# Side work of a scan held in queues: a bidirectional RWKV-7 and convolution layer on one core

## The chip, the cores and the metric

The kernel runs on one core of a Trainium2 chip. The metric is the device time of one execution in microseconds, as the median of several runs. TensorE multiplies into PSUM, ScalarE and VectorE read PSUM and SBUF, GpSimd helps with small products, and SyncE issues all DMAs of the part in question in order. Each engine works through its own list of instructions in order.

## What is computed

A layer of a diffusion backbone, 2048 tokens behind a prefix of 256 context tokens, 1024 channels, 16 heads of 64. Two branches run on the same normalized input: RWKV-7 time mixing, scanned forward and backward, and a Conformer convolution with 31 taps.

```python
def wkv_scan(s0, r, w, k, v, a_vec, b_vec, reverse, inclusive):
    def step(s, inp):
        rt, wt, kt, vt, at, bt = inp
        sa = jnp.einsum('bhij,bhj->bhi', s, at)
        s_new = s * wt[:, :, None, :] + sa[..., None] * bt[:, :, None, :] + vt[..., None] * kt[:, :, None, :]
        y = jnp.einsum('bhij,bhj->bhi', s_new if inclusive else s, rt)
        return s_new, y
...
def conformer_conv(glu_in, conv_w, conv_b, cln_w, cln_b):
    u, g = jnp.split(glu_in, 2, axis=-1)
    z = u * jax.nn.sigmoid(g)
    z = lax.conv_general_dilated(z, conv_w[:, None, :], window_strides=(1,),
                                 padding=[(CONV_K // 2, CONV_K // 2)],
                                 dimension_numbers=('NWC', 'WIO', 'NWC'),
                                 feature_group_count=WIDTH_B) + conv_b
    return jax.nn.silu(layernorm(z, cln_w, cln_b))
...
    y_a = rwkv_readout(y_sum, prep, r_k, lnx_w, lnx_b).astype(p.dtype) * jax.nn.silu(g_a)
    y_b = conformer_conv(glu, conv_w, conv_b, cln_w, cln_b) * jax.nn.silu(g_b)
    merged = jax.nn.sigmoid(m_a) * (y_a @ w_proj_a) + jax.nn.sigmoid(m_b) * (y_b @ w_proj_b)
    return merged @ w_out
```

The result is x plus a gate times this, normalized once more.

## The kernel before

**Ahead of the scan** the kernel projects the input for the scan (two fp16 halves of each operand, three matmuls for each product) and lays the operands of the scan's chunks out in DRAM (bkD, arD, vD, TA, TB).

**The scan** goes over 8 head pairs; each has 36 chunks of 64 tokens, handled forward (d = 0) and backward (d = 1) at once, in 9 groups of four. That makes 72 groups and 288 steps; a step is one call of chunk. Its chain: px from the state SV and arz; ScalarE copies it to xs; px again from xs and Tt; ScalarE copies it to UV (two halves); psy from UV and BK, one for each direction; VectorE adds it to the decayed state, four SV updates; and the next step's px needs these. One step behind, scores_out emits four output matmuls (py), whose results go to y.

**Work that fills the gaps.** prep reads a group's operands one group ahead and makes its transposes (pbk, pvt, copied by ScalarE to BK, SV, UV) and its scores (psc, masked by VectorE to arz and sc). fill_gen projects the GLU inputs and the remaining gates (pg: 24 matmuls of 512 columns to a tile), loading a weight tile at a time: wf by DMA, sum of squares on ScalarE (wjk, wss), a one-column matmul (pf), a power of two on VectorE (p2f, p2t, p2x, p2s), then whi on ScalarE and wlo on VectorE. conv_gen is the convolution on VectorE, one 128x512 instruction a tap (accq, acc). readout normalizes the outputs of a pair (pc, pv, sqy).

**The last part of the scan.** At step 236 (NEND = 288 x 0.82) the fill ends and conv_branch takes its place: for each of four blocks of 512 tokens, conv_norm (the layer norm: zc loaded, muz its mean, qsz its squares, rsz the factor, then activation and gate), split (scale, xhi, xlo) and eight tiles of the projection proj (pp, 24 matmuls each, with weights wHb and wLb), each evacuated by VectorE with the gate mb and stored to mgD. norm_split(i + 1) is pulled between the matmuls of block i. Then the weights wa and the scan's outputs ya are loaded, and the same follows with wHa; the rest of that and the output projection (po) stand behind the scan.

**What sets the order.** The program is written out by Python generators. A planner's clock for each of TensorE, VectorE and ScalarE (class Clocked) adds a modelled time for every instruction; until(t) pulls fill (at most 30 pulls) as long as TensorE's clock is behind the time at which t is ready; conv_steps emits taps until VectorE's clock is some limit ahead; pieces advances prep by a count; each generator emits its ScalarE and VectorE work where it stands. The listings below show the order in the built program.

The lines that the steps of the prediction follow:

```python
        S.activation(xs, px[:, 0:2, :], AF.Copy)
        scores_out()
...
        pieces(2 * c)
        conv_steps(LIMB)
        until(UV)
...
        conv_steps(LIM)
        pieces(2 * c + 1)
        until(Sn)
...
                        if max(clk["act"], clk["dve"]) < clk["pe"] + LIMN:
                            next(nrm, None)
```

Of the kernel before, what the change touches and what calls it, by code (L numbers as in the profile page):

```python
# [17 lines left out]
P = 128  # L18
# [26 lines left out]
LIMN = 500  # L45
# [4 lines left out]
NPC = 12  # L50
TFL = (2, 1, 2, 3)
GF = 6
# [27 lines left out]
def kernel(ctx, tc, x, xT, cc, pp, w_in, w_mod, w_lora, w_pa, w_pb, w_out, fnw, bmg, out):  # L80
# [694 lines left out]
    rdy, wrt = {}, {}  # L775
# [13 lines left out]
    class Clocked:  # L789
# [3 lines left out]
        def __getattr__(self, f):  # L793
            fn = getattr(self._e, f)

            def call(*a, **kw):
                aps = [q for q in list(a) + list(kw.values()) if is_ap(q)]
                out, ins = (kw["out"], aps) if "out" in kw else (aps[0], aps[1:])
                t = max([clk[self._n]] + [rdy.get(key(q), 0.0) + 35 for q in ins if wrt.get(key(q)) != self._n])
                n = fsz(out)  # L800
# [16 lines left out]
                else:  # L817
# [3 lines left out]
                    rdy[key(out)] = t + d + 17  # L821
                return fn(*a, **kw)  # L822
            return call

    V, S, PE = Clocked(V, "dve"), Clocked(S, "act"), Clocked(PE, "pe")
    NSTEP = NPAIR * 9
    sf = ctx.enter_context(ExitStack())
    pG = pool(ctx, "pG", 2, psum=True)
# [7 lines left out]
    pX = pool(sb, "pX", 1, psum=True)  # L836
    pS = pool(sb, "pS", 2, psum=True)
    pY = pool(sb, "pY", 1, psum=True)
    pC = pool(sb, "pC", 2, psum=True)
# [18 lines left out]
    def prep(g):  # L858
# [21 lines left out]
        yield  # L880
        for d in range(2):
            pb = pC.tile([P, 4, P], F32, name="pbk", tag="pC")
            for c in range(4):
                PE.transpose(pb[:, c, :], bk[:, d, c, :], ident)
                if c in PB:
                    yield
            S.activation(BK[:, d], pb, AF.Copy)
            yield
# [3 lines left out]
            for x in (SV, UV):  # L892
                for h, hs in enumerate(H2):
                    S.activation(x[H2[1 - h], d, :, hs], pv[H2[1 - h], :, hs], AF.Copy)
                yield
            ps = [pC.tile([P, 4, 2, 64], F32, name="psc", tag="pC") for _ in range(2)]
            ni = 1 if s == 0 else 2
            for c in range(4):
                for h, hs in enumerate(H2):
                    PE.matmul(ps[h][:, c, :ni, :], bk[hs, d, c, :], ar[hs, d, c, :ni, h, :], start=True, stop=True)  # L900
            for h in range(2):
# [4 lines left out]
            yield  # L906
# [4 lines left out]
    def readout(p, *ii):  # L911
        rs = []
        for i in ii:
            pc = pC.tile([P, 512], F32, name="pc", tag="pC")
            PE.matmul(pc, cen, ys[i], start=True, stop=True)
            S.activation(ys[i], pc, AF.Copy)
            yield
            sq = bp.tile([P, 512], F32, name="sqy")
            S.activation(sq, ys[i], AF.Square)
            rs.append(sq)  # L920
            yield
        for sq in rs:
            pv = pC.tile([P, 512], F32, name="pv", tag="pC")
            PE.matmul(pv, bones, sq, start=True, stop=True)
            S.activation(sq, pv, AF.Ln, scale=1.0 / 64, bias=eps[:, 2:3])
            yield
        for sq in rs:
            S.activation(sq, sq, AF.Exp, scale=-0.5)
        yield
        for i, sq in zip(ii, rs):  # L930
            y = ys.pop(i)
# [7 lines left out]
            V.tensor_tensor(y, y, sq, op=ALU.mult)  # L939
            S.activation(y, y, AF.Identity, scale=par[:, C_LW + p:C_LW + p + 1], bias=par[:, C_LB + p:C_LB + p + 1])  # L940
            yield
            V.tensor_tensor(bo, bo, vn, op=ALU.mult)
            V.tensor_tensor(y, y, bo, op=ALU.add)
            yield
            V.scalar_tensor_tensor(y, ga, gU["ga"][:, p:p + 1], y, op0=ALU.mult, op1=ALU.mult)
            nc.sync.dma_start(yaD[p][:, sl], y)
            yield
# [7 lines left out]
    def scores_out():  # L955
        if last:
# [3 lines left out]
            if k == 27:  # L960
                rd.append(readout(p, 1, 2))
            if k == 35:
# [640 lines left out]
```

## Time and profile before

| | us |
|---|---|
| median of 3 runs | 4117.45 (4108.43 to 4132.17) |
| profiled execution | 4115.85 |
| its span | 4114.1 |
| TensorE busy in the span | 3802.2 (92%) |
| VectorE busy | 2950.5 (72%) |
| ScalarE busy | 2181.7 (53%) |

The profile is of one execution. Busy time of TensorE counts a matmul from its start to its modelled end, and these overlap, so a full engine and one with short waits look alike there; starts of consecutive matmuls show more. The table of windows gives the busy time of each engine in a stretch, with the number of instructions in brackets and the clock that TensorE was granted (1.00 is 2.4 GHz, 0.50 is 1.2 GHz). A gap in brackets behind a timeline row is the idle time of its engine and who ended it.

### The profile page before, as it was taken

Reading aid. Unit: us, or ns where it says so; the run is one execution under the profiler, and the core shown is the slowest. Engines: PE = TensorE matmul, PEld = TensorE weight load, DVE = VectorE, ACT = ScalarE, POOL = GpSimd, SP = SyncE. Lnnn points to the kernel's source line nnn. Section 1 sums busy time; section 2 is a strip of 40 time slices with the busy share of each in tenths; the row PEclk is TensorE's granted clock in tenths of the full one; section 3 lists DMA queues with packets and bytes.
Section 4 is the critical chain, followed back from the end, with each engine's and each line's share of the span. In section 5 each row is a group of like instructions: output and inputs, shape, how many; then the busy total and the mean of one; then the engine's idle time right before and its main releaser. Section 6 shows DMA issues by size and latency. Waiting matters only on the chain. (4 is left out here: it accounts for less than half of the span.)

```text
span 4114.1 us, 78249 instructions
## 1 busy us (share of the span) xinstructions
PE 3802.2 (92%) x29008; PEld 2254.8 (55%) x29008; DVE 2950.5 (72%) x7226; ACT 2181.7 (53%) x4356; POOL 356.8 (9%) x874
## 2 busy tenths in 40 slices
PE   7999999999999897999999999999999989898999
PEld 3444444444444443676666666666676655564444
DVE  5578788687778868768696869977765566754644
ACT  5666665666666554445445454455446546544522
POOL 0000000000000000111111111111111100010000
PEclk9999999999999999999999999999999999999999
DMA  5344443444444333444444433434554555546532
GB/s 205 127 165 144 157 162 134 140 149 157 146 150 162 134 137 115 92 81 115 88 107 96 113 87 82 124 86 104 118 125 116 139 160 126 148 107 203 163 101 75
DMA packets 586116, 528.68 MB, mean 129 GB/s; under 512 B 375044, under 2 KB 439940, under 8 KB 585224
## 3 DMA queue, kind: packets, MB, share of 16 engines
q1 hardware_dynamic: 585736, 523.68, 44.2%
q8 instruction: 231, 3.78, 0.4%
q14 instruction: 149, 1.22, 0.1%
HBM read 298.01 MB, written 196.35 MB: 120 GB/s over the span
## 5 line engine op out<-in xcount | busy, mean ns | idle before, releaser
L822 DVE SCALAR_TENSOR_TENSOR SV<-psy,PL,pre 64x64 f32<-64x64 f32 x1120 | 315.8, 282 | 187.7 <-PE psy L822 168.1
L1013 POOL TENSOR_SCALAR pre<-SV,PL 128x128 f32<-128x128 f32 x560 | 290.0, 518 | 1780.1 <-DVE SV L822 1708.0
L822 PE MATMUL pg<-hH,whi 128*128 128x512 f16 x864 | 336.1, 389 | 5.7 <-ACT whi L822 4.0
L822 PE MATMUL pg<-hH,wlo 128*128 128x512 f16 x864 | 335.6, 388 | 0.4 <-DVE wlo L822 0.3
L822 PE MATMUL pg<-hL,whi 128*128 128x512 f16 x864 | 335.8, 389 | 0.0
L822 DVE SCALAR_TENSOR_TENSOR acc<-z,cw,acc 128x512 f32<-128x512 f32 x464 | 331.7, 757 | 2.7
L212 PE MATMUL pg<-hH,whi 128*128 128x512 f16 x832 | 319.0, 385 | 4.7 <-ACT hH L282 4.5
L213 PE MATMUL pg<-hL,whi 128*128 128x512 f16 x832 | 319.7, 384 | 0.1
L214 PE MATMUL pg<-hH,wlo 128*128 128x512 f16 x832 | 319.2, 384 | 0.0
L822 ACT ACTIVATE xs<-px 128x256 f32<-128x256 f32 x288 | 109.3, 380 | 383.1 <-PE px L822 381.5
L822 PE MATMUL psc<-arz,bk 64*128 64x128 f32 (+1 forms) x2304 | 259.5, 293 | 14.7 <-ACT UV L822 7.1
L822 ACT ACTIVATE UV<-px 64x128 f32<-64x128 f32 x576 | 156.1, 271 | 211.7 <-PE px L822 207.0
L363 PE MATMUL pg<-hH,whi 128*128 128x512 f16 x672 | 259.9, 387 | 2.4 <-ACT whi L203 2.4
L363 PE MATMUL pg<-hL,whi 128*128 128x512 f16 x672 | 259.4, 386 | 0.0
L363 PE MATMUL pg<-hH,wlo 128*128 128x512 f16 x672 | 258.7, 385 | 0.7 <-DVE wlo L204 0.7
L822 PEld LDWEIGHTS <-whi 128*128 128x128 f16 x1728 | 172.8, 101 | 149.7 <-issue 20.2
L822 PEld LDWEIGHTS psc<-arz,bk 64*128 64x128 f32 x2304 | 211.7, 192 | 65.9 <-issue 13.3
L822 PE MATMUL px<-SV,arz 128*128 128x128 f32 x1152 | 222.8, 297 | 24.8 <-DVE SV L822 22.9
L822 PEld LDWEIGHTS px<-SV,arz 128*128 128x128 f32 x1152 | 181.9, 195 | 84.5 <-issue 29.3
L822 PE MATMUL psy<-UV,BK 128*128 128x128 f32 x1120 | 200.4, 300 | 25.6 <-ACT UV L822 23.2
L822 PE MATMUL px<-xs,Tt 128*128 128x128 f32 x1152 | 194.7, 292 | 29.4 <-ACT xs L822 28.3
L822 DVE TENSOR_TENSOR arz<-psc,msk 64x256 f32<-64x256 f32 x288 | 120.5, 419 | 140.7 <-PE psc L822 137.1
(376 smaller groups left out, 8704.2 us busy)
## 6 DMA issues: line engine op xcount, KB each, us to landing
wf<-in_w_in_dram SPq DMA_DIRECT2D x74, 512.0 KB, 3.8
arz<-arD SPq DMA_DIRECT2D x144, 256.0 KB, 4.9
bkD<-bk SPq DMA_DIRECT2D x64, 512.0 KB, 2.7
arD<-ar SPq DMA_DIRECT2D x64, 512.0 KB, 3.5
bk<-bkD SPq DMA_DIRECT2D x72, 256.0 KB, 3.8
bk<-bkD SPq DMA_DIRECT2D x144, 128.0 KB, 3.9
vvz<-vD SPq DMA_DIRECT2D x144, 128.0 KB, 2.9
lt<-loD SPq DMA_DIRECT2D x32, 512.0 KB, 4.9
```

The source lines that it names most:

```text
L212: PE.matmul(ps, whi[:, k, :], xhi(k), start=(k == 0), stop=False)
L213: PE.matmul(ps, whi[:, k, :], xlo(k), start=False, stop=False)
L214: PE.matmul(ps, wlo[:, k, :], xhi(k), start=False, stop=(k == NK - 1))
L363: PE.matmul(ps, wt[a][:, k, :], b[:, k, o:o + 512], start=(m == 0), stop=(m == 23))
L822: return fn(*a, **kw)
L1013: G.tensor_scalar(pr, SV[:, d, c, :], pl, 1.0, op0=ALU.mult, op1=ALU.mult)
```

## The change

Side work is taken out of the places where its generator emits it and held in two queues, qA (ScalarE) and qD (VectorE); outputs of the scan in yA and yD. chunk empties them at two places: behind the emission of UV, and behind the four SV updates. prep is cut into pieces of kind "B" (a transpose with its copy) and "C" (scores), which are called by kind at these two places; so are readout's steps. Loading a weight tile becomes four small queue entries (a1, d1, a2, d2); its one-column matmul takes a buffer of psy's pool. A wrapper around the PSUM pools (Slots) tells the planner's clock when a buffer is free again. If two pg buffers are open, free_pg empties all queues at once. In the last part of the scan, conv_norm and split no longer run between the matmuls of proj; they stand in a list bg that chunk advances. GF (gate tiles between the GLU tiles) goes from 6 to 8.

```diff
-LIMN = 500
+LIMN = 800
+LIMM = 700
+LIMQ = 2600
...
+                if self._n == "pe":
+                    t = max(t, war.get(key(out), 0.0))
...
+    def run_q(q, eng, lim):
+        i = 0
+        while i < len(q) and clk[eng] < clk["pe"] + lim:
+            f = q.pop(i)
+            if f(lim > 1e8) is False:
+                q.insert(i, f)
+                i += 1
...
         if c == 0 and prv[0] is not None:
-            next(prv[0], None)
+            kind[0] = next(prv[0], None)
         until(xs)
...
-        pieces(2 * c)
+        run_y(yA)
+        run_q(qA, "act", LIMQ)
+        run_q(qD, "dve", 100)
+        pieces("B", c)
         conv_steps(LIMB)
         until(UV)
...
         rdy[key(Sn)] = max(s0_, rdy[key(Sn)] - 224)
+        run_y(yD)
+        run_q(qD, "dve", LIMQ)
+        run_q(qA, "act", 500)
+        pieces("C", c)
+        while bg and max(clk["dve"], clk["act"]) < clk["pe"] + LIMN:
+            if next(bg[0], 1) == 1:
+                bg.pop(0)
         conv_steps(LIM)
-        pieces(2 * c + 1)
         until(Sn)
...
+        yield "B"
+        turn(0)
+        yield "C"
+        scores(0)
+        yield "B"
+        values(0)
...
+    def free_pg():
+        if cnt["pg"] >= 2:
+            force()
+        cnt["pg"] += 1
...
+        def d1(f):
+            if clk["pe"] < rdy[key(ss)] + 35 and not f:
+                return False
+            pf = pS.tile([P, P], F32, name="psy")
+            PE.matmul(pf[:, 0:1], ones, ss, start=True, stop=True)
+            sc = pow2(wp2, pf[:, 0:1], 1)
+            qA.append(lambda f: a2(sc))
...
+            bg.append(norm_split(0))
             for i in range(4):
-                x3 = c_["x3"]
-                nrm = norm_split(i + 1) if i < 3 else iter(())
+                while ("x3", i) not in c_:
+                    yield
+                x3 = c_["x3", i]
+                if i < 3:
+                    bg.append(norm_split(i + 1))
                 for ct in range(NK):
                     mb = tmp()
                     nc.sync.dma_start(mb, mbD[ct][:, 512 * i:512 * (i + 1)])
-                    pr = proj(wb, ct, x3, cw_, pG, "pG")
-                    while True:
-                        try:
-                            next(pr)
-                        except StopIteration as ex:
-                            ps, un = ex.value
-                            break
-                        if max(clk["act"], clk["dve"]) < clk["pe"] + LIMN:
-                            next(nrm, None)
-                        yield
...
+                    free_pg()
+                    ps, un = yield from proj(wb, ct, x3, cw_, pG, "pG")
...
     while "first" not in c_:
         next(cb, None)
+        force()
+        if bg and next(bg[0], 1) == 1:
+            bg.pop(0)
+    force()
```

pull, which until calls, is not changed: while conv_branch runs, it returns true whenever the generator yields, also if it emitted nothing.

**TensorE in the middle of the scan, step 130.** First before, then after; the names are those of the chain and of prep above, pg with whi and wlo the gate work.

```order
L822 MATMUL px<-SV_18650,arz_18648 128x128 x2
L822 MATMUL py<-arz_18648,SV_18650 128x128
L822 MATMUL py<-sc,UV 128x128
L822 MATMUL py<-arz_18648,SV_18650 128x128
L822 MATMUL py<-sc,UV 128x128
L822 MATMUL px<-xs,Tt_18646 128x128 x2
L822 MATMUL psc<-arz_18649,bk 128x128 x8
L822 MATMUL psy<-UV,BK 128x128 x2
L822 LDWEIGHTS whi
L822 MATMUL pg<-hL,whi 128x512
```

```order
L827 MATMUL px<-SV_18650,arz_18648 128x128 x2
L827 MATMUL py<-arz_18648,SV_18650 128x128
L827 MATMUL py<-sc,UV 128x128
L827 MATMUL py<-arz_18648,SV_18650 128x128
L827 MATMUL py<-sc,UV 128x128
L827 MATMUL px<-xs,Tt_18646 128x128 x2
L827 MATMUL pvt<-ident,vvz 128x128 x4
L827 MATMUL pbk<-ident,bk 128x128 x4
L827 MATMUL psy<-UV,BK 128x128 x2
L827 LDWEIGHTS whi
L827 MATMUL pg<-hL,whi 128x512
```

The transposes now stand between px and psy; the eight scores went behind psy, six pg matmuls further on.

**TensorE in the last part of the scan, steps 253 to 255.** Before, the end of step 255's cover and its psy; after, two whole steps and the start of the third. pp with wHb and wLb is the conv projection.

```order
L822 LDWEIGHTS wLb
L822 MATMUL pp<-xhi,wLb 128x512
L822 LDWEIGHTS wHb
L822 MATMUL pp<-xhi,wHb 128x512
L822 MATMUL px<-xs,Tt_18647 128x128 x2
L822 MATMUL psc<-arz_18648,bk 128x128 x8
L822 MATMUL psy<-UV,BK 128x128 x2
L822 LDWEIGHTS wHb
L822 MATMUL pp<-xlo,wHb 128x512
```

```order
L827 MATMUL px<-SV_18651,arz_18649 128x128 x2
L827 MATMUL px<-xs,Tt_18647 128x128 x2
L827 MATMUL pbk<-ident,bk 128x128 x4
L827 MATMUL psy<-UV,BK 128x128 x2
L827 MATMUL px<-SV_18651,arz_18649 128x128 x2
L827 MATMUL px<-xs,Tt_18647 128x128 x2
L827 MATMUL psc<-arz_18648,bk 128x128 x4
L827 MATMUL psy<-UV,BK 128x128 x2
L827 MATMUL px<-SV_18651,arz_18649 128x128 x2
```

No pp stands between the steps any more; all 768 of them now come behind the last px.

**VectorE in the conv norm of a later block.** Before, inside the scan; after, behind it. tc<-pp is the evacuation of a projection tile, SV the scan's state, y and bo the readout.

```order
L822 TENSOR_TENSOR zc<-zc,muz 128x512 x4
L822 TENSOR_TENSOR bo<-bo,vn 128x512
L822 TENSOR_TENSOR qsz<-qsz,tc_36369 128x512
L822 TENSOR_TENSOR y<-y,bo 128x512
L822 TENSOR_TENSOR qsz<-qsz,tc_36402 128x512
L822 SCALAR_TENSOR_TENSOR y<-ga,gUga,y 128x512
L822 TENSOR_TENSOR qsz<-qsz,tc_36406 128x512
L822 TENSOR_TENSOR zc<-zc,muz 128x512
L822 SCALAR_TENSOR_TENSOR tc_36300<-pp,unp,tc_36300 128x512
```

```order
L827 TENSOR_TENSOR zc<-zc,muz 128x512
L827 TENSOR_TENSOR qsz<-qsz,tc_38055 128x512
L827 SCALAR_TENSOR_TENSOR tc_37995<-pp,unp,tc_37995 128x512
L827 TENSOR_TENSOR qsz<-qsz,tc_38060 128x512
L827 TENSOR_TENSOR unp<-wpU_246,p2s 128x1
L827 TENSOR_TENSOR qsz<-qsz,tc_38064 128x512
L827 SCALAR_TENSOR_TENSOR tc_38077<-pp,unp,tc_38077 128x512
L827 TENSOR_TENSOR unp<-wpU_246,p2s 128x1
L827 TENSOR_TENSOR zc<-zc,rsz 128x512 x5
```

The norm of the next block now stands in one piece between the evacuations of two tiles, with no scan work among it.

## Rows read from the trace of the kernel before

**Rows 1.** The head of the profile's page: the span.

```profile
span 4114.1 us, 78249 instructions
```

**Rows 2.** Windows: us; busy (count) PE, PEld, DVE, ACT, POOL; clock; DMA; GB/s.

```profile
1676.00:1811.00 135.00, 130.23 (x879) 101.74 (x879) 116.50 (x269) 61.98 (x176) 29.08 (x53) 1.00 0.45 89
1811.00:3300.00 1489.00, 1395.77 (x9057) 994.52 (x9056) 1117.97 (x2723) 747.86 (x1738) 217.73 (x431) 0.97 0.45 106
3300.00:3746.00 446.00, 399.94 (x2393) 271.70 (x2390) 276.17 (x669) 228.85 (x522) 44.11 (x100) 0.93 0.54 141
3746.00:3757.00 11.00, 7.59 (x16) 3.66 (x17) 3.25 (x17) 7.54 (x16) 0.00 (x0) 0.69 0.89 277
3757.00:4114.00 357.00, 337.11 (x1554) 152.69 (x1553) 188.62 (x411) 125.08 (x283) 0.00 (x0) 0.98 0.38 126
```

**Rows 3.** TensorE's waits, 1811 to 3300: total us, times, longest.

```profile
PE psy L822 <- ACT UV L822: 17.8, 31, 1.7
PE px L822 <- DVE SV L822: 17.0, 29, 3.0
PE px L822 <- ACT xs L822: 15.7, 26, 2.2
```

**Rows 4.** Groups on TensorE, 1811 to 3300: count | busy, mean ns | idle before.

```profile
L822 PE MATMUL pg<-hL,whi 128*128 128x512 f16 x775 | 301.5, 389 | 0.0
...
L822 PE MATMUL pv<-sqy,bones 128*128 128x512 f32 x48 | 25.3, 608 | 2.3 <-DVE sc L822 2.3
```

**Rows 5.** Timeline of steps without projection work: start us, us, engine, what.

```profile
3737.49 0.71 PE L822 MATMUL psy<-UV,BK 128*128 128x128 f32 x4 [0.64 <-ACT UV L822]
...
3738.09 1.19 DVE L822 SCALAR_TENSOR_TENSOR SV<-psy,PL,pre 64x64 f32<-64x64 f32 x4 [4.29 <-PE psy L822]
...
3738.26 0.39 PE L822 MATMUL py<-arz,SV 128*128 128x128 f32 x2
...
3738.49 0.39 PE L822 MATMUL py<-sc,UV 128*128 128x128 f32 x2
...
3738.81 1.01 PE L822 MATMUL px<-SV,arz 128*128 128x128 f32 x4
...
3739.92 0.38 ACT L822 ACTIVATE xs<-px 128x256 f32<-128x256 f32 x1 [2.48 <-PE px L822]
...
3740.36 0.71 PE L822 MATMUL px<-xs,Tt 128*128 128x128 f32 x4 [0.53 <-ACT xs L822]
...
3741.71 0.71 PE L822 MATMUL psy<-UV,BK 128*128 128x128 f32 x4 [0.65 <-ACT UV L822]
...
3743.41 0.46 PE L822 MATMUL px<-SV,arz 128*128 128x128 f32 x2
```

**Rows 6.** Timeline of TensorE inside a projection tile, two consecutive matmuls.

```profile
3767.60 0.38 PE L822 MATMUL pp<-xlo,wHa 128*128 128x512 f16 x1
3767.82 0.38 PE L822 MATMUL pp<-xhi,wLa 128*128 128x512 f16 x1
```

**Rows 7.** Groups on TensorE, 3300 to 3746: one of three of the conv projection.

```profile
L822 PE MATMUL pp<-xhi,wHb 128*128 128x512 f16 x256 | 100.8, 395 | 0.4 <-ACT xhi L822 0.4
```

**Rows 8.** Instructions on tile zc, 3300 to 3650: ns min/median/max, first and last.

```profile
L822 DVE TENSOR_TENSOR zc<-zc,rsz x24: 680/685/693, 3362.4 to 3586.8; 128x512 f32<-128x512 f32 x24
...
L822 DVE TENSOR_SCALAR zc<-zc,hcl x24: 536/544/604, 3365.5 to 3609.8; 128x512 f32<-128x512 f32 x24
L822 DVE SCALAR_TENSOR_TENSOR zc<-tc,zc x24: 672/684/693, 3366.5 to 3610.9; 128x512 f32<-128x512 f32 x24
L822 DVE SCALAR_TENSOR_TENSOR zc<-tc,gUgb,zc x24: 730/744/752, 3367.6 to 3625.6; 128x512 f32<-128x512 f32 x24
```

**Rows 9.** Timeline around the norm's factor rsz.

```profile
3358.45 1.02 PE L822 MATMUL pva<-qsz,ones 128*128 128x512 f32 x2
...
3362.45 1.90 DVE L822 TENSOR_TENSOR zc<-zc,rsz 128x512 f32<-128x512 f32 x3 [0.22 <-ACT rsz L822]
```

**Rows 10.** Window in which wa and ya are loaded; columns as in rows 2.

```profile
3713.00:3733.00 20.00, 16.39 (x101) 13.16 (x100) 10.71 (x30) 14.11 (x25) 1.88 (x4) 0.91 0.91 329
```

More of the change, by code (lines that the diff above doesn't have):

```diff
@@ L1057, in conv_gen, with tap @@
             q = zp.tile([P, 512], F32, name="accq", bufs=1)
-            S.activation(q, z[:, 1, b:b + 512], AF.Identity, scale=hs01[:, 0:1], bias=par[:, C_CB + ct:C_CB + ct + 1])
+            first = []
+            def tap(f, q=q, b=b, first=first):
+                S.activation(q, z[:, 1, b:b + 512], AF.Identity, scale=hs01[:, 0:1], bias=par[:, C_CB + ct:C_CB + ct + 1])
+                first.append(1)
+            qA.append(tap)
+            while not first:
+                yield "wait"
             for j in range(1, n0):
@@ new lines, in gate4, with g1, g2 @@
+    def gate4(nm, ct, wt, un):
+        for i in range(4):
+            free_pg()
+            pg = pG.tile([P, 512], F32, name="pg", tag="pG")
+            yield from gemm_parts(wt, TC + 512 * i, pg, NSUB)
+            def g1(f, pg=pg, i=i):
+                tg = f5()
+                S.activation(tg, pg, AF.Tanh, scale=un)
+                def g2(f):
+                    if nm[0] == "g":
+                        V.scalar_tensor_tensor(tg, tg, 1.0, pg, op0=ALU.add, op1=ALU.mult)
+                        if i == 0:
+                            V.tensor_copy(gU[nm][:, ct:ct + 1], un)
+                    else:
+                        V.tensor_scalar(tg, tg, 0.5, 0.5, op0=ALU.mult, op1=ALU.add)
+                    nc.sync.dma_start(gdst[nm][1][ct][:, 512 * i:512 * (i + 1)], tg)
+                    cnt["pg"] -= 1
+                qD.append(g2)
+            qA.append(g1)
+            yield
@@ L1163, in fill_gen @@
-            for m, _ in enumerate(u):
-                if m + 1 in (NSUB, 2 * NSUB, 3 * NSUB):
-                    next(ah, None)
-                yield
-            for _ in ah:
-                pass
-    def unit4(nm, ct, wt, un, i):
-        yield from gate_unit(nm, ct, wt, un, i, pG, "pG", f5, NSUB)
-        yield
+            yield from (glu_tile(ct, wu, wt) if nm == "wg" else gate4(nm, ct, wt, un))
+        while busy or jobs2:
+            loader()
+            force()
+        force()
@@ L1405, in until, with pieces @@
             n += 1
-    def pieces(gap):
-        if rd and next(rd[0], 1) == 1:
-            rd.pop(0)
-        want = max(0, gap - 1) * NPC // 6
-        while prv[0] is not None and cnt["pc"] < want:
-            cnt["pc"] += 1
-            next(prv[0], None)
+    kind = [None]
+    def pieces(kd, c):
+        if rd:
+            if rk[0] is None:
+                rk[0] = next(rd[0], 1)
+            if rk[0] == kd:
+                rk[0] = next(rd[0], 1)
+            if rk[0] == 1:
+                rd.pop(0)
+                rk[0] = None
+        n = {"B": (0, 1, 2, 1), "C": (0, 1, 1, 0)}[kd][c]
+        while n > 0 and prv[0] is not None and kind[0] == kd:
+            for _ in range(MAXP):
+                if clk["pe"] >= pC.free() or not pull():
+                    break
+            kind[0] = next(prv[0], None)
+            n -= 1
+    rk = [None]
+    cb = None
     cb = None
@@ L1448 @@
     scores_out()
+    force()
     for r in rd:
```

311 lines of the change are left out of this document (188 added, 123 removed).

## The prediction

> **What bounds the kernel now.** I first split the profiled execution, whose span is 4114.1 us [rows 1], into stretches by the table of busy time per window [rows 2]. The scan is 72 groups of four steps, 288 steps; the first and the last matmul of px put it from 1676 to 3746 us, and counting the px groups puts step 24 at 1811 us and step 236 at 3300 us. Before step 236 the steps are filled with gate and GLU matmuls (pg), after it with the 768 matmuls of the conv projection (pp).
>
> TensorE shows busy for 1396 of the 1489 us of the long stretch [rows 2], but matmuls overlap, so I count what they need: two consecutive pp start 0.22 us apart (call it 0.216), and two short fp32 ones take 0.22 us, so 0.11 each [rows 5, 6]. Of the 9057 matmuls there [rows 2], 2323 are pg (three groups of 774 or 775), 96 are the long fp32 ones of the readout (four short ones each, 0.44 us), the other 6638 are short [rows 4]: 502 + 42 + 730, minus some 8 because the 76 one-column ones are shorter, is about 1265 us. So 1489 - 1265 = 224 us are neither needed nor hidden. The granted clock, 0.97 [rows 2], means that 6% of the stretch, 89 us, ran at 1.2 GHz; that costs about half, 45 us. The other 180 us are waits, and the list of waits names them: psy for UV, px for SV, px for xs [rows 3], the chain of a step. (The list counts only gaps beyond the modelled ends, hence its smaller sums.)
>
> The chain itself is short. In a step without projection work [rows 5] px starts at 3738.81 and again on xs at 3740.36; px occupies 0.45 us, so 1.10 us of other matmuls hide the copy xs. From there to psy at 3741.71 it is 1.35, so 0.90 us hide UV; from psy at 3737.49 over SV to px at 3738.81 it is 1.32, so 1.10 us after the first psy hide SV. The sum, 3741.71 - 3737.49 = 4.22 us, is the least that a step takes, against 1489/212 = 7.0 us. So before step 236 TensorE's work is the bound, and what can be won are the 180 us of waits and the 45 of clock.
>
> **The change, part by part.** *Steps 24 to 236.* Work on TensorE is the same to 2 us by the counts of the order. Where it stands differs: after puts four py behind px, the transposes before psy and the eight scores behind it. I added up, over these 212 steps, how much the cover falls short of 1.10, 0.90 and 1.10 us: 51 + 17 + 6 = 73 us before, 45 + 8 + 1 = 54 after, a gain of 19. The remaining 180 - 73 = 107 us are waits where the cover would do but ScalarE, VectorE or a PSUM buffer is late; the queues put side work behind UV and SV instead of ahead, and prep's matmuls wait for a free buffer in the planner's clock. No row prices that. Its bounds are 0 and 107 us; I take half, 50, since the VectorE side work is unchanged in amount (1118 of 1489 us busy [rows 2]) and one conv instruction still can't be interrupted. Fewer waits also mean less low clock: 16 of 45 us. Together -85 us, with bounds -19 and -150.
>
> *Start of the scan.* Before has some 46 pg ahead of the first px, after has none there and more in steps 10 to 24: px starts 7 us sooner and the first 24 steps take as much more. Nil. The weight loads in small steps, the sum of squares in psy's pool (41 matmuls of one column), the conv tap in ScalarE's queue, GF and the two mean matmuls in pC are inside the counts above; I cost them at nothing more, since the long stretch's pg work hides them, and 10 us if it doesn't.
>
> *Steps 236 to 288.* Here the order decides. Before, all 768 pp stand between the steps. After, none does: the first follows the last px. The code says why. The norm and split of a column block now sit in the list bg, advanced only behind psy, where chunk has just emitted four SV updates, and only if the clocks of VectorE and ScalarE are less than 800 ns ahead of TensorE's. With no projection work to move TensorE's clock this holds almost never; conv_branch spins on its own yield, and the 30 pulls of a wait return without a matmul. So 51 steps run bare. Streaming what they keep takes 184 us; the shortfalls against 1.10, 0.90 and 1.10 us add 38 + 25 + 11; readout work on ScalarE and VectorE and a lower clock I put at 30, as much as these cost in the same stretch of before (446 - 355 needed - 24 short = 67 with norm work, about half without it). 288 us, against 446 [rows 2]: -158, call it -160. Bounds: 51 x 4.22 = 215 us (-231) and, with all at 1.2 GHz, 12 short matmuls of chain at 0.11 us more, 51 x 1.3 = 66 us more (-92).
>
> *Behind the scan* stand now 768 pp, 768 x 0.216 = 166 us, which [rows 7] shows inside the scan, and three of the four norms. The order on VectorE is serial with them: of each block the evacuations of tiles 4 to 7, then norm, then tiles 0 and 1, then the scaling and the split; PSUM has two buffers for pp, so tile 2 waits for tile 0, and TensorE has the two mean matmuls in line. From one block's scale matmul to the next one's: four tiles, 4 x 24 x 0.216 = 20.7, plus about 4 for two late evacuations; 13 matmuls and the mean matmul, 4.6; fifteen subtractions and additions at 0.685 and two evacuations at 0.744, 11.8 [rows 8]; variance matmul, Ln, table load and Exp until VectorE goes on, 3362.45 - 3358.45 = 4.0 [rows 9]; eight times 0.685 + 0.544 + 0.684 + 0.744, 21.3; last square, sum, matmul, 1.5. That is 68 us, of which TensorE needs 41. The first block comes to 60 (no tiles ahead, but the load of zc), the last to 25 + 41: 60 + 68 + 68 + 66 = 262, and 8 for the clock that falls in the gaps. Then SyncE: the loads of wa (4 MB) and ya (2 MB) stand behind the last store of the projection. At the 329 GB/s of the window in which before loads them [rows 10] that takes 19 us, and squares, scale and split 6 more before the first pp of wa: 25, which before lay beside steps of the scan; 3 for the cold clock behind it. Between the last px and the first pp I take 18 us instead of 11 [rows 2], for four table loads of the readout ahead of xhi. So behind the last px there are 18 + 270 + 28 + 357 = 673 us, against 11 + 357 = 368: +305. Bounds: +175 if everything but pp were hidden, +340.
>
> Sum on the span: 4114 - 85 - 160 + 305 = 4174. The profiled execution took 4115.85 us, 1.75 over its span, and stands 1.6 under the median of 4117.45; I predict 4176 us.
>
> On the clock: rows 2 show 1.00 at the start of the scan, where TensorE has hardly a gap, 0.93 in steps 236 to 288, which already hold the longest waits, and 0.69 in the 11 us after it, where TensorE stood. The Trainium skill, "TensorE: Matmul & The Clock Gate", section "A second HAM failure mode: psum-queue depth-cycling", says that frequent small idle spells between groups of matmuls make the clock swing between its two levels even without a long stop. The trace agrees in direction, and by that rule the bare steps would come out as in the fourth rival below; no run here shows a bare stretch of that length.
>
> **The rivals.** *Forecast*: the cover taken from the last 51 steps costs more behind the scan than the steps give back: 4176, 4140 to 4230 by its own bounds.
>
> *Faster*: the chain really runs free. Then steps 24 to 236 lose 150 us, the bare steps take 215 (-231), and behind the scan it is +290: 4114 - 150 - 231 + 290 = 4023, 4025 with what lies around. For it: the regular order of after. Against it: VectorE is 75% busy [rows 2], and in the very step of [rows 5] the next px came 1.70 us behind psy instead of 1.32 (3743.41 - 3741.71), late by a readout instruction. It decides when the two gains exceed 305 us together.
>
> *Even*: both gains good but not full, -120 and -185: 4116.
>
> *Half clock*: the gaps of the bare steps and of the blocks behind drop TensorE to 1.2 GHz for most of that time: +55 and +10, 4240. For it: the 0.93 and 0.69 above. Against: with prep's matmuls the bare steps still keep TensorE streaming for 184 of 288 us.
>
> *The change doesn't do what it says*: side work is as late as before, because a forced emptying of the queues (at a third open pg buffer) emits all of it at once. Then steps 24 to 236 gain only 19: 4176 + 66 = 4242.
>
> **How the numbers follow.** Forecast 0.58, half clock 0.10, no better queues 0.12, even 0.13, faster 0.07. About 0.5%, 20 us, is what a measurement of this kernel can tell from no change. Slower by more than that hold the forecast, half clock and no better queues: 0.80; within it the even case: 0.13; faster 0.07. The range, 4110 to 4265, takes in the even case at the low end and both dearer ones with their own spread at the high end; it leaves out the faster one and the ends of the bounds.
>
> **What would show it.** In the trace of the changed kernel: no pp before the last px, and the last px near 3500 instead of 3746 (first step near 1669, long stretch near 1405, bare steps near 288, 5.6 us each); behind it pp in bursts with TensorE idle some 16 us per block ahead of the scale matmul, waiting in the end for VectorE's zc; idle of about 25 us ahead of the first pp of wa, ended by a load; the last 357 us unchanged. Waits of px and psy in the long stretch should be about half. I am wrong if the long stretch falls under 1340 us, if the bare steps take 4.5 us or 7, or if the blocks behind the scan take 45 us each, that is, if TensorE and not VectorE bounds them.

## The result, and the profile of the changed kernel

The changed kernel took 4246.31 us (median of 4 runs, 4237.04 to 4254.98), the kernel before 4113.84 in the same comparison: a ratio of 1.0314, 95% interval 1.0273 to 1.0354. Slower, as forecast, but by 132 us and not by 59. The head of the page of the changed kernel, then its windows, cut where rows 2 were (scan start, step 24, step 236, last step, first pp of wa); columns as in rows 2:

```profile
span 4241.7 us, 78338 instructions
```

```profile
1670.00:1830.00 160.00, 144.04 (x891) 110.55 (x892) 99.79 (x254) 67.69 (x183) 23.31 (x48) 0.88 0.45 93
1830.00:3249.00 1419.00, 1359.41 (x9083) 979.28 (x9082) 1114.01 (x2710) 720.79 (x1716) 203.54 (x436) 0.99 0.47 108
3249.00:3591.00 342.00, 262.22 (x1599) 216.88 (x1597) 152.73 (x426) 158.57 (x388) 38.50 (x98) 0.87 0.43 87
3591.00:3885.00 294.00, 191.50 (x810) 84.12 (x809) 157.77 (x304) 103.51 (x178) 0.00 (x0) 0.84 0.44 144
3885.00:4241.00 356.00, 339.20 (x1554) 153.44 (x1553) 184.76 (x415) 117.55 (x275) 0.00 (x0) 0.98 0.34 113
```

Against [rows 2]: the first row is longer and its clock fell from 1.00 to 0.88; the second is shorter; the third is much shorter, at 0.87; the fourth, 294 us, is what was 11 us; the last is the same. TensorE's waits between 1830 and 3249 us (total us, times, longest), to set beside [rows 3]:

```profile
PE px L827 <- ACT xs L827: 15.1, 15, 2.6
PE psy L827 <- DVE SV L827: 14.6, 18, 1.8
PE px L827 <- DVE SV L827: 6.1, 14, 1.5
...
PE psy L827 <- ACT UV L827: 4.0, 10, 0.8
```

The three waits of the chain fell from 50.5 to 25.2 us. The new row, psy for SV, is the weight loading's one-column matmul (psy<-wss), which now needs a buffer of psy's pool.

Counting the copies xs gives step times without windows that cut a step. All kernels of this study, from their traces (us; the first step's xs, steps 0 to 24, 24 to 236, 236 to the last, from the last xs to the end, span) with the time of the run or the median. norm0_spread, bare_dummy_norm0 and the six from own_pull_now to own_pull_gf6 were run once, so their times have no interval; the others are medians of 4 to 10 runs:

| kernel | xs 0 | 0-24 | 24-236 | 236-287 | behind | span | time |
|---|---|---|---|---|---|---|---|
| before | 1679.6 | 131.8 | 1489.7 | 443.4 | 369.6 | 4114.1 | 4113.84 |
| changed | 1670.0 | 160.5 | 1418.8 | 341.9 | 650.4 | 4241.7 | 4246.31 |
| before_list | 1677.0 | 131.8 | 1488.7 | 331.8 | 649.5 | 4278.8 | 4274.9 |
| before_weights | 1677.6 | 159.0 | 1438.2 | 439.4 | 366.3 | 4080.5 | 4083.62 |
| own_pull | 1678.1 | 158.3 | 1418.3 | 438.5 | 387.2 | 4080.4 | 4083.3 |
| own_all | 1670.4 | 161.8 | 1418.0 | 438.5 | 387.2 | 4075.8 | 4080.42 |
| limit_2200 | 1669.8 | 160.7 | 1443.4 | 339.6 | 505.4 | 4118.9 | 4122.55 |
| limit_5000 | 1671.4 | 160.5 | 1431.4 | 415.3 | 400.1 | 4078.7 | 4084.1 |
| bare_dummy | 1672.9 | 158.4 | 1414.8 | 314.2 | 650.1 | 4210.4 | 4214.89 |
| norm0_spread | 1668.6 | 160.5 | 1426.4 | 331.0 | 647.8 | 4234.3 | 4236.01 |
| bare_dummy_norm0 | 1671.9 | 160.5 | 1422.8 | 293.9 | 649.3 | 4198.5 | 4200.24 |
| own_pull_now | 1684.0 | 142.6 | 1516.1 | 435.5 | 390.7 | 4169.0 | 4170.74 |
| own_pull_now2 | 1671.3 | 158.8 | 1411.6 | 433.2 | 391.2 | 4066.1 | 4067.85 |
| own_pull_pieces | 1673.3 | 161.8 | 1414.9 | 443.0 | 390.4 | 4083.4 | 4085.09 |
| own_pull_nowar | 1670.2 | 158.0 | 1427.0 | 440.1 | 390.0 | 4085.3 | 4087.0 |
| own_pull_onepiece | 1671.4 | 169.0 | 1474.8 | 438.5 | 390.6 | 4144.4 | 4146.1 |
| own_pull_gf6 | 1682.3 | 159.0 | 1410.6 | 437.5 | 387.4 | 4076.8 | 4078.55 |
| best_18 | 1680.0 | 142.9 | 1420.0 | 424.4 | 370.4 | 4037.7 | 4039.46 |
| best_20 | 1680.1 | 143.2 | 1420.2 | 430.4 | 367.2 | 4041.1 | 4045.7 |
| best_limit | 1674.0 | 142.9 | 1425.3 | 405.0 | 393.3 | 4040.5 | 4041.99 |

Before to changed: -10, +29, -71, -101 and +281, together the 128 us of the spans. Where two kernels are the same up to some step, their stretches differ by up to 4 us (own_pull and own_all: 158.3 and 161.8, 1418.3 and 1418.0) and the first xs by up to 10 (norm0_spread and own_pull: 1668.6 and 1678.1); smaller differences are not read here.

### The profile page after: what moved, and what is told of

Same layout as the page of the kernel before. It is cut to its first block, busy times and chain, and to the rows that moved or that the text cites. A ratio compares the mean times of both kernels' runs of the same rounds, so it can differ in the third digit from the quotient of the medians.

```text
span 4241.7 us, 78338 instructions
## 1 busy us (share of the span) xinstructions
PE 3821.6 (90%) x29008; PEld 2274.6 (54%) x29008; DVE 2949.0 (70%) x7226; ACT 2174.8 (51%) x4358; POOL 331.5 (8%) x874
## 4 chain that ended last, share of the span: by engine, by line
PE 51%; DVE 29%; ACT 12%; issue 5%; DMA 3%; SPq 0%; DVEq 0%; ACTq 0%
PE pg L827 8%; PE pp L827 7%; PE px L827 6%; PE psc L827 5%; PE py L827 4%; PE po L827 4%; DVE X L480 4%; DVE tmp L479 3%; PE psy L827 3%; DVE acc L827 3%; PE pg L364 2%; ACT UV L827 2%; DVE SV L827 2%; DVE zc L827 1%; PE pg L215 1%
## 5 line engine op out<-in xcount | busy, mean ns | idle before, releaser
L1070 POOL TENSOR_SCALAR pre<-SV,PL 128x128 f32<-128x128 f32 x560 | 264.8, 473 | 1655.6 <-DVE SV L827 1468.0
L827 PE MATMUL psc<-arz,bk 64*128 64x128 f32 (+1 forms) x2304 | 277.0, 293 | 19.6 <-ACT UV L827 13.7
L827 PEld LDWEIGHTS psc<-arz,bk 64*128 64x128 f32 x2304 | 231.2, 193 | 81.8 <-ACT UV L827 36.2
```

Source lines behind the costliest of these rows:

```text
L1070: G.tensor_scalar(pr, SV[:, d, c, :], pl, 1.0, op0=ALU.mult, op1=ALU.mult)
```

## Experiments: the list of the conv branch

**own_pull** lets the conv branch advance its own norm again:

```diff
                 while ("x3", i) not in c_:
-                    yield
+                    if bg and next(bg[0], 1) == 1:
+                        bg.pop(0)
+                    yield from pause(YS)
...
+                        if bg and max(clk["act"], clk["dve"]) < clk["pe"] + 500:
+                            if next(bg[0], 1) == 1:
+                                bg.pop(0)
+                        yield
```

> The changed kernel, with one part undone: the conv branch again advances its norm and split itself, between the matmuls of its projection and while it waits for a block, as before; queues, pieces and the clock for PSUM buffers stay. In the built order all 768 pp then stand inside the scan again. Theory (the whole loss is this list, which starves in the last 52 steps): those steps and what is behind the last px come back to before's 443 and 370 us, the rest keeps its +19 and -71: 4114 - 71 + 19 = 4062 us. Rival (VectorE's side work is late because of the queues, wherever norm and split are advanced): at least 4150 us. If it lies between 4075 and 4140, the list is most of it and the queues cost something in the last steps too.

Ratio 0.9925 (0.9911 to 0.994): 4083.3 us, 21 over the theory. The last steps are back at 438 us, the rest behind at 387, not 370. The remaining 18 us are one wait, the split of ya; first before, then here:

```profile
PE pfs L822 <- DVE s__39451 L822: 4.7, 1, 4.7
...
PE pfs L827 <- DVE s__39127 L827: 22.2, 1, 22.2
```

**before_list** puts that list alone into the kernel before (norm_split and the split of ya in bg, advanced behind the state updates; the norm's mean matmuls move to the PSUM pool pC, as in the changed kernel):

```diff
+        while bg and max(clk["dve"], clk["act"]) < clk["pe"] + 800:
+            if next(bg[0], 1) == 1:
+                bg.pop(0)
         conv_steps(LIM)
```

> The kernel before, with that one part of the change alone: norm and split of the conv branch stand in the list that a step advances behind its four state updates, if VectorE's and ScalarE's clocks are less than 800 ns ahead. No queues. In the built order no pp is inside the scan. Theory (the list alone is the loss): 101 us less in the last 52 steps and 281 more behind them, as measured for the change: 4114 + 180 = 4294 us, slower than the changed kernel by the 52 us that its other parts won. Rival (the list starves only together with the queues' side work): under 4170 us.

Ratio 1.0392 (1.0374 to 1.0409): 4274.9 us. Its last steps and what is behind them, by windows:

```profile
3297.00:3629.00 332.00, 272.90 (x1597) 226.33 (x1596) 126.95 (x380) 145.48 (x368) 38.96 (x99) 0.85 0.40 87
3629.00:4278.00 649.00, 533.44 (x2364) 238.09 (x2363) 341.59 (x716) 221.15 (x453) 0.00 (x0) 0.91 0.38 126
```

The list does the whole damage without any queue: 112 us won in the steps, 280 lost behind them. With own_pull this shows the cause from both sides.

**limit_2200** and **limit_5000** change one number of the changed kernel:

```diff
-LIMN = 800
+LIMN = 2200
```

> The changed kernel with the limit at 2200 ns: in the built order 402 of the 768 pp stand inside the scan. Theory (time follows the number of pp that stand behind the scan): of the 281 us behind the last px 366/768 stay, 134, and of the 101 us won in the last 52 steps 402/768 are given back, 53: 4246 - 147 + 53 = 4152 us. Rival (it is the norms' serial work and not the place of pp that counts): near 4246 as long as one norm is left behind the scan, so 4200 or more.

> The changed kernel, with one number changed: the list is advanced while VectorE and ScalarE are less than 5000 ns ahead instead of 800. In the built order all 768 pp stand inside the scan. Theory (the limit starves the list): the tail shrinks to about 370 us again and the last 52 steps go to about 443: 4062 us, as with the part undone. Rival (a norm that is emitted in pieces of up to 5 us behind the state updates makes the next step's updates late, so the gain is spent in the steps): 4110 to 4160 us.

4122.55 us (1.0025, 1.0015 to 1.0034) and 4084.1 us (0.9931, 0.9916 to 0.9945). So the limit starves the list. limit_5000 stays 22 us over its theory; in its trace the stretch ahead pays 13 us and the part behind the scan 30, and the last steps give back 28. limit_2200's last 52 steps:

```profile
3274.00:3613.00 339.00, 313.09 (x1986) 230.94 (x1987) 222.52 (x567) 187.72 (x446) 47.06 (x98) 0.96 0.53 123
```

With 402 pp among them these steps take 339.6 us, with none 341.9: the expected 53 us were not given back, and though the stretch ahead paid 25 (1443.4 against 1418.8), the time is 30 us under the expected 4152. The two stretches are not alike, though: here norm 0 is done earlier, in the stretch that paid, and steps 236 and 237 take 8.0 and 5.9 us instead of the 12.6 and 24.4 that the next section comes to. Over the 49 steps behind these two it is 325.7 us against 304.9: the 402 pp, 87 us of streaming at 0.216, and the norms among them cost 21.

**own_all** also drives the split of ya from the branch:

```diff
-        bg.append(mix_split(ORDER[0]))
-        while bg:
-            yield
+        yield from slow(mix_split(ORDER[0]))
```

> As own_pull, and the split of ya (the scan's outputs, for the projection with wa) is driven by conv_branch too and no longer by the list. In own_pull's trace TensorE stands 22.8 us between 3703.9 us and the scale matmul behind the scan, and the part behind the last px is 386.3 us instead of before's 368.7. Theory (that is the same starvation, of the list's last entry): 386 goes to 369, so 4083 - 18 = 4065 us. Rival (the wait is the load of ya behind the stores of the projection, whoever issues it): 4083 us, unchanged.

The rival held: 387.2 us behind, unchanged. In own_all's trace the load of wa is issued at 3686.3 us, 2 us ahead of the last xs; in the kernel before it was 31 us ahead of it (3713.3 and 3744.5). The projection ends some steps too late: its last pp stands 8 us ahead of the last xs, in the kernel before 33.

## Experiments: the bare steps

In the changed kernel steps 236 and 237 take 12.6 and 24.4 us, the other 49 take 6.2 on the mean. First VectorE, then TensorE around 3264 us (start, us, engine, what, idle before):

```profile
3264.33 3.10 DVE L827 TENSOR_TENSOR zc<-zc,rsz 128x512 f32<-128x512 f32 x5 [4.38 <-ACT rsz L827]
...
3278.25 0.28 DVE L827 SCALAR_TENSOR_TENSOR SV<-psy,PL,pre 64x64 f32<-64x64 f32 x1
...
3283.58 0.60 DVE L827 SCALAR_TENSOR_TENSOR SV<-psy,PL,pre 64x64 f32<-64x64 f32 x2
```

```profile
3284.01 0.77 PE L827 MATMUL px<-SV,arz 128*128 128x128 f32 x2 [16.32 <-DVE SV L827]
```

The end of the fill emits the rest of norm 0 in one piece; the state updates stand behind it, and TensorE waits 16.3 us. **norm0_spread** advances this norm with the fill:

```diff
-                bg.append(conv_norm(0, f5))
+                nrm0.append(conv_norm(0, f5))
+            if nrm0:
+                if ny % NRS == 0:
+                    next(nrm0[0], None)
+                ny += 1
             yield
```

> The changed kernel, with the norm of the first conv block advanced at every 14th pull of the fill as before, and no longer held in the list. In the changed kernel's trace that norm's rest is emitted in one piece at step 236, and steps 236 and 237 take 12.6 and 24.3 us where the others of the last 52 take 6.2. Theory (the piece stands on VectorE ahead of the state updates): both steps come to 6 to 8 us, the last 52 to about 318 instead of 342 us, and steps 24 to 236 gain no more than 8: 4246 - 20 = 4226 us. Rival (VectorE is full in the steps ahead of 236 too, so the norm's work costs there what it saves here): 4240 to 4250 us.

**bare_dummy** adds matmuls whose results nobody uses; the list is not advanced while they run:

```diff
             cnt["cb"] += 1
+            if bare:
+                PE.matmul(bare[0], bare[1][:, 0, 0, :], bare[1][:, 1, 0:4, :].rearrange("p k c -> p (k c)"), start=True, stop=True)
             return next(cbs[0], 1) is None
```

> The changed kernel, with matmuls that do nothing useful in the last 52 steps: wherever the planner finds TensorE waiting there, it emits matmuls of 128x512 on a loaded weight tile into an unused PSUM buffer, 309 in all, 67 us of streaming. Theory (the bare steps take 6.7 us instead of the 5.6 forecast because TensorE falls to 1.2 GHz there, 92 of 342 us): with the clock up the 51 steps take 342 - 46 = 296 us or a little more, 4246 - 40 = 4206 us. Rival (the steps wait for ScalarE's and VectorE's side work, readout and the norm's rest, and the clock only follows): the clock is near 1.0 but the steps stay at 330 to 350 us, 4246 us; if the dummies come late themselves, up to 4290 us.

**bare_dummy_norm0** is both.

> bare_dummy and norm0_spread together: idle matmuls of no use wherever the planner finds TensorE waiting in the last 52 steps (309), and norm 0 advanced with the fill. Theory (low clock and the norm in one piece are all that stands between the forecast 288 us and the measured 342): the 49 steps behind 237 took 5.66 us each with the dummies, so 51 take 289 us. Rival (the two share one loss; norm0_spread took only 11 us off 342 and the dummies 28): 303 us or more.

norm0_spread took 4236.01 us: step 237 falls to 7.6 us, but step 236 stays at 11.9, since instructions of the norm (zc) still stand among its state updates on VectorE. The stretch lost 11 us, and the one before it paid 8. bare_dummy: 1.0276 (1.0254 to 1.0297), 4214.89 us, the stretch 28 us shorter for 67 us more work. Its window, then that of both together:

```profile
3246.00:3560.00 314.00, 292.69 (x1900) 215.13 (x1899) 150.96 (x422) 156.53 (x387) 38.51 (x98) 0.99 0.44 93
```

```profile
3255.00:3549.00 294.00, 277.59 (x1891) 216.00 (x1891) 137.85 (x400) 144.80 (x368) 41.80 (x99) 0.97 0.46 99
```

VectorE and ScalarE do the same work as in the changed kernel (151 against 153, 157 against 159 us), the clock goes from 0.87 to 0.99. That fits a loss to the clock, but does not show it alone: the dummies also move the planner's clock, and in the trace the order of the other matmuls and of the side work in these steps is no longer that of the changed kernel. Nor do the steps of one trace decide it. Of the 49 steps behind 237, those at full clock throughout took 5.69 us on the mean in the changed kernel and the others 7.14; in norm0_spread it is 6.56 and 6.06. Clock and order were not separated.

Together 293.9 us, between the two expectations and 6 over the forecast 288: the two changes win 48 of the 54 us. Step 236, still 11.8 us here, holds the other 6.

## Experiments: where the gain of steps 24 to 236 comes from

**own_pull_now** emits each queue entry where it is appended; **own_pull_now2** does so for all but the weight loading:

```diff
+    class Now(list):
+        def append(self, f):
+            if f(True) is False:
+                list.append(self, f)
...
-    qA, qD, bg = [], [], []
+    qA, qD, bg = Now(), Now(), []
```

> As own_pull, but the four queues emit each entry where it is appended, as far as its operands are there, as the kernel before did; pieces by kind and the clock for PSUM buffers stay. Theory (the 71 us won in steps 24 to 236 come mostly from the queues): that stretch goes from 1418 us to 1465 or more. Rival (they come from the place of prep's pieces and the PSUM clock): at most 1435 us. In the built order steps 0 to 8 hold as many pg as before again (78 by step 12, where own_pull has 24): if the missing fill is what costs the first 24 steps 27 us, they go from 158 to about 132 us; if not, they stay.

> own_pull_now, but the weight loading's four entries stay in the queues until their data are there; all other side work (evacuations of pg and py, the tap, gates) is emitted where it is appended. own_pull_now's stretch of steps 24 to 236 took 1516 us, with 60.8 us of waits of a one-column matmul for wjk. Theory (the queues of the other side work are worth what is left, 98 - 61 = 37 us): 1418 + 37 = 1455 us. Rival (only the held weight loading matters): 1418 to 1428 us. In the built order the first 24 steps hold no more pg than in own_pull, so 158 us there either way; if it comes to 143, the missing pg are not what made them slow.

own_pull_now seemed to show that the queues are worth 98 us. Its first wait says otherwise:

```profile
PE psy L827 <- ACT wjk L827: 60.8, 15, 12.0
```

That is the weight loading, emitted ahead of its data. With only that held back, own_pull_now2 takes 1411.6 us, 7 less than with all queues. The queues of the other side work give nothing here. The first 24 steps of own_pull_now, which hold 79 pg by step 12 and not 25, take 142.6 us, between the 132 of its expectation and the 158 of own_pull; own_pull_now2, without these pg, takes 158.8.

**own_pull_pieces** advances prep by one piece a place, whatever its kind; **own_pull_nowar** takes the PSUM buffers out of the planner's clock; **own_pull_gf6** sets GF back to 6:

```diff
-        n = {"B": (0, 1, 2, 1), "C": (0, 1, 1, 0)}[kd][c]
-        while n > 0 and prv[0] is not None and kind[0] == kd:
+        n = 1 if c > 0 else 0
+        while n > 0 and prv[0] is not None:
...
-            war[key(t)] = self.free()
```

> own_pull, but prep's six pieces are advanced one at each place from the second step of a group on, whatever their kind, as the count of before did, so that scores can stand ahead of psy and transposes behind it. Theory (cover ahead of psy, the prediction's 19 us, and evacuations at the wrong place): steps 24 to 236 go from 1418 to 1437 us or more. Rival (the place of the pieces is worth nothing as long as pg fills the gaps): within 6 us of 1418.

> As own_pull, but the planner's clock does not know when a PSUM buffer is free. Theory (queues and pieces give the gain in steps 24 to 236): 1418 us there rises by less than 15. Rival (matmuls that wait for a buffer in the midst of a chain were the gain): 1445 us or more.

> own_pull with six instead of eight gate tiles between the GLU tiles, as in the kernel before. Theory (only the order of tiles changes): steps 24 to 236 stay within 8 of 1418 us. Rival (the taps of the convolutions come too early with six and hold up VectorE): 1440 us or more.

1414.9, 1427.0 and 1410.6 against 1418: nothing, 9 us, and 8 us the other way, each from one run.

**own_pull_onepiece** holds a weight tile until it has landed and then emits all of it at once; **before_weights** puts the changed weight loading, with its two queues, alone into the kernel before:

```diff
-            qD.append(d1)
+            d1(True)
...
-            qA.append(lambda f: a2(sc))
+            a2(sc)
...
-            qD.append(lambda f: d2(sc, hi))
+            d2(sc, hi)
```

> own_pull, with the weight loading held only until its tile has landed; then sum of squares, one-column matmul, power of two, whi and wlo are emitted in one piece. Theory (small steps give the gain: ScalarE, waiting for VectorE's power of two ahead of whi, holds up xs and UV): steps 24 to 236 go from 1418 to 1450 us or more. Rival (it is enough that the loading waits for its data and keeps out of pg's two buffers): under 1430.

> The kernel before with the changed weight loading alone: one tile at a time, four small entries held in the two queues until their data are there, the one-column matmul in a buffer of psy's pool, not of pg's. Evacuations, tap, outputs, pieces and the conv branch are those of before. Theory (the weight loading gives the gain of steps 24 to 236, and takes the loss of the first 24): 1490 goes to 1430 or less, the first 24 steps from 132 to 158, the rest stays: 4114 - 60 + 26 = 4080 us. Rival (the gain needs the parts together): 1465 us or more there, 4105 or more.

own_pull_onepiece: 1474.8 us, 56 more, and the wait for wjk is back, while that for xs did not grow (15.1 us in own_pull):

```profile
PE psy L827 <- ACT wjk L827: 29.0, 14, 6.3
PE px L827 <- ACT xs L827: 13.2, 15, 2.4
```

So the theory's sum held and its mechanism did not: TensorE stands at the one-column matmul, for 29 of the 56 us. The granted clock of the stretch is 0.980 instead of 0.994, which is 58 us at 1.2 GHz instead of 17; if such time costs half of itself, as the prediction reckons, that is another 20 (an estimate).

before_weights: 4083.62 us, ratio 0.9947 (0.9924 to 0.997):

```profile
1678.00:1836.00 158.00, 142.78 (x897) 109.55 (x897) 101.55 (x267) 69.69 (x184) 22.65 (x47) 0.90 0.45 96
1836.00:3275.00 1439.00, 1355.50 (x9088) 964.42 (x9086) 1137.69 (x2736) 743.97 (x1734) 216.41 (x437) 0.99 0.46 107
```

Alone it gives 51 of the 71 us, and all of the start's loss: 159.0 us for the first 24 steps, with the same missing pg in the built order. Of the other 20, about 8 are norm 0, which stood in this stretch before (norm0_spread pays them back); the rest is not pinned to a part, and own_pull_nowar's 9 us are the only candidate. Its waits of the chain from 1831 to 3244 us, to set beside [rows 3]:

```profile
PE px L836 <- ACT xs L836: 13.6, 22, 2.5
PE px L836 <- DVE SV L836: 10.9, 18, 1.3
...
PE psy L836 <- ACT UV L836: 10.3, 28, 1.1
```

34.8 us instead of 50.5 (34.4 in the stretch as the table cuts it). In the kernel before, TensorE's own wait at the one-column matmul was small (1811 to 3300 us):

```profile
PE pf L822 <- ACT wjk L822: 7.8, 8, 1.8
```

So most of the 51 us are not that wait. A part goes with the clock, 0.9893 over the stretch here and 0.9725 before: 31 us of it ran at 1.2 GHz and not 82, by the same reckoning 26 us (an estimate). By which engine the old loading held up the chain, or by taking one of pg's two buffers, was not separated.

## Experiments: repairs

**best_18** is own_all with norm 0 spread, the queues emitting at once in the first 24 steps, and 18 pulls a step; **best_20** has 20; **best_limit** is limit_5000 with the start and 20 pulls:

```diff
+    class Soon(list):
+        def append(self, f):
+            if cnt["n"] >= 24 or f(True) is False:
+                list.append(self, f)
...
-MINCB = 16
+MINCB = 18
```

> own_all with three repairs: the queues emit at once in the first 24 steps (own_pull_now's 142.6 us there instead of 158), norm 0 is advanced with the fill, and each of the last 52 steps takes at least 18 pulls of the projection instead of 16, so that it ends at step 281 as in the kernel before and wa can load inside the scan. Theory (these are the three places where own_pull at 4083 us still lost): -16, -20 and -17, so 4030 us. Rival (VectorE, 75% busy in the last 52 steps, makes them longer by what the norm and the wait for wa gave): 4060 us or more.

> As best_18 with at least 20 pulls a step: in the built order the projection ends at step 277. Theory (only the load of wa has to be in time): as best_18, 4030 us within 8. Rival (the bare steps at the end are cheap, 5 us, and denser ones ahead cost more than their pp): 4045 us.

> limit_5000 with the queues emitting at once in the first 24 steps and at least 20 pulls in each of the last 52; the list stays and also carries norm 0. limit_5000 took 415 us for the last 52 steps and 399 behind the last px. Theory (the start gives 16, the earlier load of wa up to 20): 4084 - 36 = 4048 us. Rival (the projection ends only at step 284, too late for the load, and the split of ya is still in the list): 4068 us.

best_18: 4039.46 us, ratio 0.9826 (0.9808 to 0.9844), 9 us over its theory; best_20 0.9844 (0.982 to 0.9868), best_limit 0.9831 (0.9813 to 0.9848). The three intervals overlap, so best_18 is not shown to be the fastest. Its windows:

```profile
1680.00:1823.00 143.00, 134.74 (x887) 101.39 (x886) 115.93 (x270) 62.00 (x177) 24.52 (x52) 0.98 0.44 90
1823.00:3243.00 1420.00, 1360.37 (x9078) 980.82 (x9076) 1101.79 (x2684) 730.72 (x1734) 203.19 (x432) 0.99 0.47 108
3243.00:3667.00 424.00, 387.75 (x2374) 263.89 (x2374) 288.10 (x691) 223.15 (x516) 50.51 (x98) 0.96 0.57 151
3667.00:4037.00 370.00, 345.70 (x1576) 156.72 (x1574) 191.76 (x429) 133.74 (x302) 0.00 (x0) 0.97 0.39 131
```

Against own_pull and own_all the first 24 steps gave about 17 us (but the first xs came 2 and 10 us later), norm 0 and the shorter projection 14, and the load of wa, issued at 3640.4, 27 us ahead of the last xs, the 17 behind. An earlier load of wa alone does not do it: best_limit keeps 393 us behind although its load starts 12 us ahead of the last xs, and own_pull_now 391 with 18 us; whether the rest is the load of ya or the list was not separated.

## Why the prediction was right in direction and wrong in size

**Behind the scan**, +305: +281. Right, 24 too much. From the last xs to the first pp 16.8 us (18 taken), the 768 pp 254.1 (270), to the first pp of wa 24.7 (28), the rest 354.8 (357). TensorE in the second block behind the scan:

```profile
3628.58 2.07 PE L827 MATMUL pmu<-muz,ones 128*128 128x512 f32 x2 [3.30 <-DVE muz L827]
3640.88 2.07 PE L827 MATMUL pva<-qsz,ones 128*128 128x512 f32 x2 [10.23 <-DVE qsz L827]
3666.93 0.58 PE L827 MATMUL pfs<-s__37764,ones 128*128 128x1 f32 x2 [17.60 <-DVE s__37764 L827]
```

17.6 us of idle ahead of the scale matmul, ended by VectorE, and 14.9 in each of the two blocks behind: the 16 that were named. VectorE bounds these blocks.

**Steps 236 to 288**, -160: -101. This is the step that failed, and the largest error, 58 us. Its sentence "readout work on ScalarE and VectorE and a lower clock I put at 30" took the clock from a stretch of before whose gaps pp had filled, and the sum has no term for the rest of norm 0 at steps 236 and 237. The measured 342 us leave 84 where 30 stood: 48 of them go when matmuls fill the gaps and norm 0 is spread (bare_dummy_norm0), with clock and order not separated, and 6 stay in step 236. The 5.6 us a step are right where neither acts: with the dummies the 49 steps behind 237 took 277.3 us, 5.66 each, and with both 274.6. The bound of -92 held.

**Start**, nil: +19 (first xs 10 us sooner, 24 steps 29 longer). The failed step is "I cost them at nothing more, since the long stretch's pg work hides them": at the start there is no pg yet, because pg is what waits for the weights. With one tile at a time, held until its data are there, steps 0 to 8 hold no pg, and the clock falls to 0.88. (All 24 steps hold 37 more pg than before, 8 us of streaming, as the forecast had them move; the rest of the 29 us it did not have.) That the loading does it is shown: before_weights has it alone, and 159.0 us. With pg there again, best_18 takes 142.9 for these steps, but its first xs comes 10 us later, so 11 or 12 of the 19 us stay open.

**Steps 24 to 236**, -85: -71, inside its bounds, for the wrong reason: that it came so close is luck. I gave 19 us to the cover ahead of psy, 50 to the queues, 16 to the clock and nothing to the weight loading. (The shortfalls of the kernel before add up to 74, not 73, which moves nothing.) Pieces and queues are worth nothing, the weight loading 51 to 56, its share of the clock included. The waits of [rows 3] name who was late, SV, UV and xs, and not what made them late; 16 of the 25 us by which they fell came from a part of the change that touches none of the three (before_weights).

The four errors, +19, +14, +58 and -24, make the 67 us between the forecast span of 4174 and 4241.7.

**The rivals.** Half clock gave 4240, close to the result, but its mechanism is a part only: the granted clock was 0.87 and 0.84 where it speaks of half, and the matmuls that lifted it in the steps won 28 us, not 55. The Trainium skill, "TensorE: Matmul & The Clock Gate", section "A second HAM failure mode: psum-queue depth-cycling", names frequent small idle spells between groups of matmuls as what makes the clock swing in a kernel measured there; the runs agree, since useless matmuls in such gaps bring it from 0.87 to 0.99. No better queues, 4242, was right on the queues and wrong on the stretch, since another part won it. Faster and even did not come: they needed 305 us or more from the two gains, which gave 172.

## What to carry to other kernels

A side branch that advances only "when the other engines are not far ahead" must be checked for the case in which nothing moves the clock it is compared with: here 768 matmuls slid out of steps that took 112 us less without them, to a place where they and their norms took 280 (before_list). Work that fills waits costs much less there than its streaming time (limit_2200: 21 us where 87 are streamed), and the granted clock rose with it, so take it out last. And before crediting a mechanism with a gain, put it alone into the old kernel: most of this one came with the new weight loading, to which the forecast gave nothing.

## What the runs showed of the hardware

Adding 67 us of useless matmuls to steps full of short waits made them 28 us shorter, at a granted clock of 0.99 instead of 0.87 (the order of the side work changed with them). And one column of a matmul emitted ahead of its data cost 60.8 us in 15 waits, the longest 12.0 us, since everything behind it on TensorE waited too (own_pull_now, whose stretch took 98 us more than own_pull's).
